# A gate pair with three Strassen units in place of four, one-piece splits of x1, a fourth raw weight tile

## Chip, cores and metric

One core of one Trainium2 chip. The metric is device time in microseconds (us), the median of several runs of the same program; the profile is of one further execution.

## The reference

One layer of a hybrid decoder block on 256 tokens of width 2048, all in float32:

```
h  = RMSNorm(x);  u = h @ w_in                     # 2048 x 12288, cut into c b xa za q f iv og ga gb
ya = b * conv3(c * xa) * silu(za)                  # 1024 wide
yb = RMSNorm_head(HGRN2(q, f, iv)) * silu(og)      # 1024 wide, 8 heads of 128
m  = sigmoid(ga) * (ya @ w_a) + sigmoid(gb) * (yb @ w_b)
x1 = x + m @ w_o                                   # 2048 x 2048
x2 = x1 + sigmoid(RMSNorm(x1) @ w_pg) * (p @ w_pp) # w_pg: 2048 x 2048
out = RMSNorm(x2)
```

The change acts on the last two products: the end of `m @ w_o`, and `x1 @ w_pg`.

## The kernel before, in words

Each product is cut into groups of 512 output columns. A group's contraction runs over chunks of 256 rows, each two tiles of 128 rows; the 256 tokens are two halves of 128. To keep float32 precision, every operand is split into a high part (rounded to the fp32r type) and a low part (the rest), and each product is made of three matmuls: high x high, high x low, low x high (`product`, L1147; inside a pair, `add`, L1169).

*Weights* come as a raw tile of two chunks (1 MB), loaded by SyncE's queue, SP (`load`, L103), with three raw tiles in rotation. `split` (L130) then makes, chunk by chunk, `whi` with one ScalarE copy (ACT, L151) and `wlo` with one VectorE subtraction (DVE, L152). Steps of the program are numbered; `ahead(pos)` says how many steps the splits run ahead of the matmuls, and `ask_ahead` asks for raw tiles. Four split buffers rotate; in the last stage, from the first step of `w_pg` on, six more in the pool `late`.

*Groups.* After the four groups of `w_o` (kind `O`) come those of `w_pg`: group 0 by itself (`PG` 0, eight steps), groups 1 and 2 as a pair (`GP`), and group 3 (`PG` 3) at the end, in which the first token half is done over all 512 columns, and the second half in two pieces of 256 columns. In a pair a chunk for both groups can be done as a *Strassen unit* ("S", chunk): seven block products where the plain way takes eight, from sums of weight blocks (`combine_weights`, L163 to L167, in place in the raw tile and in a half tile `t2`) and sums of blocks of x1 (`forms`). It takes four parts, one of them half a step wide. A plain unit (group, chunk) takes two chunks of one group, in two parts. The order is a list written out by hand, `LATE`.

*Epilogue of the pair.* `sums` (L765) waits until all products of a bank are made and adds the banks up (L761, L774); when gate 1, then gate 2 is whole, `gated` (L902) applies sigmoid (L908), the product with the kept projection `pw` (L911), the addition to the residual (L912) and the sum of squares (L913, L920). Of the PSUM banks with tag `g` there are four; the pair holds all four, so the last group's first bank is one that the additions have read.

*The O epilogue* (`ep_o`) adds the product to the residual, and turns x1 into feature-major layout (`turned`): four writes to DRAM (L294), one read back (L296), both from SP, then DVE's transpose (L300). For groups 0 and 1 of x1, four ACT scalings, one copy and one subtraction make the high and low parts, and `forms` the block sums. For groups 2 and 3 `put` does it in four scaled copies (L258) and four subtractions (L259).

*Tail.* `last_half` (L928 to L936) handles a piece of the last group, `sums_so_far` (L945 to L957) closes the sums of squares of the pieces before, `last_norm` (L966 to L985) scales and stores.

*What sets the order.* Each engine runs its instructions in one fixed order, which a scheduler lays down when the program is built, from the program's order, the pools' buffers and its own estimates. `advance` makes the epilogues' next steps after each step of matmuls, `issue_after` puts those behind the splits already issued.

Of the kernel before, what the change touches and what calls it, by code (L numbers as in the profile page):

```python
# [15 lines left out]
P = 128  # L16
# [25 lines left out]
GATES = ("S", 0), (0, 2), ("S", 1), (1, 2), ("S", 4), (0, 6), ("S", 5), (1, 6)  # L42
LATE = (0, 4), ("S", 0), (0, 6), ("S", 1), (1, 4), ("S", 2), ("S", 3), (1, 6)

# [7 lines left out]
def hybrid_kernel(ctx, tc, xT, x, pT, prm, gfin, masks, w_in, w_a, w_b, w_o, w_pg, w_pp, out):  # L52
# [44 lines left out]
    stream = []  # L97
    unit_of, part_of, joint = [], [], []
    loaded = {}
    parts = {}  # L100
    half = {}

    def load(pos):  # L103
        w, g, c = stream[pos]
        if unit_of[pos] not in loaded:
            raw = wp.tile([P, 2, 2 * CW], F32, tag="raw", bufs=3, name=nm("raw"))
            loaded[unit_of[pos]] = raw
            if joint[pos]:
                nc.sync.dma_start(out=raw[:, 0, :], in_=w[g, :, c, :])
                for i in range(2):  # L110
                    nc.sync.dma_start(
                        out=raw[:, 1, i * CW : (i + 1) * CW], in_=w[g + 1, :, c, (1 - i) * CW : (2 - i) * CW]
                    )
            elif FIRST <= pos < FIRST + 20:
                for i in range(2):
# [14 lines left out]
    def split(pos, c0=0, c1=2 * CW):  # L130
        part = part_of[pos]
        src = load(pos)[:, part % 2, :]
        if joint[pos]:

            src = load(pos)[:, part == 3, :]
            if part == 1:
                src, c1 = half[unit_of[pos]], CW

        pool, n = (pools["late"], 6) if (pos - state.get("late", len(steps))) % 10 < 6 and "late" in state else (wp, 4)
        if more(pos) and pos % (4 + MORE) < MORE:  # L140
            pool, n = pools[more(pos)], MORE
        if pos not in parts:
            parts[pos] = tuple(
                pool.tile([P, 2 * CW], F32R, tag=tag, bufs=n, name=nm(tag)) for tag in ("whi", "wlo")
            )
        hi, lo = parts[pos]
        s = slice(c0, c1)
        with ExitStack() as order:
            for i in state["before"].pop() if state.get("before") else ():
                order.enter_context(tc.issue_after(i))  # L150
            a = nc.scalar.activation(out=hi[:, s], in_=src[:, s], func=AF.Copy)  # L151
            v = nc.vector.tensor_tensor(  # L152
                out=lo[:, s], in0=src[:, s], in1=hi[:, s].bitcast(F32), op=ALU.subtract
            )
        state["splits"] = (a.ins, v.ins)
        if joint[pos] and part == 0:
            combine_weights(pos)
# [24 lines left out]
    active, done = [], 0  # L182
    def add_step(gi, c, w, g, k, part, s):
# [4 lines left out]
        joint.append(s)  # L188

    for gi, (kind, j, w, g, op, *program) in enumerate(groups):  # L190
# [4 lines left out]
        for n, (u, c) in enumerate(program[0]):  # L195
            for part in range(4 if u == "S" else 2):
                add_step(gi, (n, part), w, g if u == "S" else g + u, c if u == "S" else c + part, part, u == "S")

# [5 lines left out]
    gates, late = of_kind("GG"), of_kind("PG")[0]  # L204
    gates = range(gates[0] - 12, gates[-1] + 9)

# [77 lines left out]

    def turned(src, lag, dst=None):

# [8 lines left out]
        yield  # L295
        nc.sync.dma_start(out=src, in_=d.rearrange("p a x -> p (a x)"))  # L296
        for _ in range(lag):
# [424 lines left out]
    def forms(op, pool, tag, r, chunks):  # L722


        f = t4()
        a11, a12, a21, a22 = (r[:, :, k, t * P : (t + 1) * P] for t in range(2) for k in range(2))
        s1, s2, s3, s4 = (f[:, i * 2 * P : (i + 1) * 2 * P].rearrange("p (u t) -> p u t", u=2) for i in range(4))
        nc.vector.scalar_tensor_tensor(out=s1, in0=a21, scalar=-1.0, in1=a22, op0=ALU.mult, op1=ALU.subtract)
# [4 lines left out]
        yield  # L733
        hi, lo = (pool.tile([P, 1024], F32R, tag=tag + x, bufs=len(chunks) // 2, name=nm(tag + x)) for x in "hl")
        nc.scalar.activation(out=hi, in_=f, func=AF.Copy)
        nc.vector.tensor_tensor(out=lo, in0=f, in1=hi.bitcast(F32), op=ALU.subtract)
        for u in range(2):
            for i in range(4):
                s = slice((2 * i + u) * P, (2 * i + u + 1) * P)
                state["S", op, chunks[u], i] = hi[:, s], lo[:, s]  # L740
# [397 lines left out]
    def ahead(pos):  # L1138

        return LEAD + min(max(pos - late - 4, 0) // 3, 5) + MORE * (more(pos + LEAD) is not None and more(pos + LEAD + MORE) == more(pos + LEAD))  # L1140

# [54 lines left out]
    def products_of(program):  # L1196

        plain = [4 * sum(u == g for u, _ in program) for g in range(2)]
        joined = sum(u == "S" for u, _ in program)
# [204 lines left out]
```

## Time and profile before

| | |
|---|---|
| runs | 815.12 us median of 3 (814.78 to 815.52) |
| profiled execution | 814.94 us |
| its span, first to last instruction | 813.1 us |
| mean granted TensorE clock | 0.997 |
| TensorE (PE) busy | 802.5 us, 4196 matmuls |
| VectorE (DVE) busy | 629.6 us |
| ScalarE (ACT) busy | 465.2 us |
| GpSimd (POOL) busy | 91.1 us |
| DMA, mean over the span | 232 GB/s |

Places in the span: the `O` groups' matmuls end at 718.4 us, `PG` 0 runs from there to about 740, the pair to 781, the last group to 804.4. A row of an order of time has start, duration, engine, line, operation, tiles, and in brackets how long the engine had stood idle and what it waited for. A group row has, behind the first bar, busy time and the mean ns of one instruction, and behind the second the idle time before them. A window's row has, after its length, busy time and count of PE, PE's weight loads, DVE, ACT and POOL, then the clock, the DMA engines' share and GB/s.

### The profile page before, as it was taken

To read this page: it belongs to the slowest core of one execution; us is meant where nothing else is said; L and a number is where in the kernel's file an instruction comes from. 1 tells how busy PE (TensorE), PEld (TensorE's weight loads), DVE (VectorE), ACT (ScalarE), POOL (GpSimd) and SP (SyncE) were. 2 spreads that over 40 slices of the span, in tenths; PEclk is the share of its full clock that TensorE was granted. 3 is DMA by queue.
4 is the path that set the end of the run, shared out by engine and by line. 5 is a ranking of instruction groups with operands and counts; after the bars stand their busy time and mean duration, and the time that the engine had idled before them with its cause. 6 is when DMAs were issued, how large, how long until landed. Compare 5 with 4: busy or idle time off the path is not lost.

```text
span 813.1 us, 10989 instructions
## 1 busy us (share of the span) xinstructions
PE 802.5 (99%) x4196; PEld 666.9 (82%) x4196; DVE 629.6 (77%) x742; ACT 465.2 (57%) x609; POOL 91.1 (11%) x74
## 2 busy tenths in 40 slices
PE   9999999999999999999999999999999999999995
PEld 7888888888888888888888888888888888888875
DVE  5747697967766488967767998998997657779996
ACT  7667475555555465565664555564564456665653
POOL 1000045400000055200001000100100000001012
PEclk9999999999999999999999999999999999999998
DMA  9979656747767555647764774774766687887442
GB/s 337 366 281 338 226 172 206 228 172 237 258 233 256 186 183 202 213 156 264 269 238 148 224 272 144 248 257 157 259 236 230 213 300 257 283 315 252 165 181 105
DMA packets 46709, 188.33 MB, mean 232 GB/s; under 512 B 5312, under 2 KB 14784, under 8 KB 31552
## 3 DMA queue, kind: packets, MB, share of 16 engines
q1 hardware_dynamic: 46512, 187.36, 66.6%
q8 instruction: 33, 0.54, 0.3%
q10 hardware_dynamic: 144, 0.26, 0.1%
q14 instruction: 20, 0.16, 0.1%
HBM read 173.97 MB, written 13.63 MB: 231 GB/s over the span
## 4 chain that ended last, share of the span: by engine, by line
PE 90%; DVE 5%; DMA 1%; issue 1%; ACT 1%; POOL 0%; ACTq 0%; POOLq 0%; DVEq 0%
PE g L1147 73%; PE g L1169 11%; PE s L1169 4%; DVE wlo L152 2%; DMA raw<-in_w_pg 1%; PE s L1147 1%; PE s L450 1%; DVE t L911 1%; DVE raw L163 1%; DMA raw<-in_w_pp 0%; DVE xs L912 0%; ACT whi L151 0%; DVE t L929 0%; DVE t L761 0%; DVE t L166 0%
## 5 line engine op out<-in xcount | busy, mean ns | idle before, releaser
L152 DVE TENSOR_TENSOR wlo<-raw,whi 128x1024 fp32r<-128x1024 f32 (+1 forms) x311 | 385.1, 1254 | 154.3 <-ACT whi L151 153.0
L151 ACT ACTIVATE whi<-raw 128x1024 fp32r<-128x1024 f32 (+1 forms) x311 | 320.8, 1049 | 251.1 <-PE g L1147 195.6
L1147 PE MATMUL g<-whi,xh 128*128 128x512 f32 (+1 forms) x656 | 251.8, 385 | 0.6 <-DVE t L761 0.6
L1147 PE MATMUL g<-wlo,xh 128*128 128x512 f32 (+1 forms) x656 | 251.9, 384 | 0.0
L1147 PE MATMUL g<-whi,xl 128*128 128x512 f32 (+1 forms) x656 | 251.7, 384 | 0.0
L1147 PEld LDWEIGHTS g<-whi,xh 128*128 128x128 f32 x656 | 123.3, 188 | 25.2 <-DVE t L761 1.0
L1147 PEld LDWEIGHTS g<-whi,xl 128*128 128x128 f32 x656 | 123.3, 188 | 24.5
L1147 PEld LDWEIGHTS g<-wlo,xh 128*128 128x128 f32 x656 | 123.3, 188 | 24.2
L1169 PE MATMUL g<-wlo,xh 128*128 128x512 f32 x160 | 62.2, 389 | 0.0
L1169 PE MATMUL g<-whi,xl 128*128 128x512 f32 x160 | 62.2, 389 | 0.0
L1169 PE MATMUL g<-whi,xh 128*128 128x512 f32 x160 | 62.1, 389 | 0.0
L1147 PE MATMUL g<-whi,mh 128*128 128x512 f32 x128 | 49.8, 389 | 0.0
L1147 PE MATMUL g<-wlo,mh 128*128 128x512 f32 x128 | 49.8, 389 | 0.0
L1147 PE MATMUL g<-whi,ml 128*128 128x512 f32 x128 | 49.6, 389 | 0.0
L151 ACT ACTIVATE whi<-t 128x512 fp32r<-128x512 f32 x16 | 10.1, 630 | 53.7 <-DVE t L166 53.7
L1169 PEld LDWEIGHTS g<-whi,xh 128*128 128x128 f32 x160 | 30.0, 188 | 6.2
L1169 PEld LDWEIGHTS g<-wlo,xh 128*128 128x128 f32 x160 | 30.0, 188 | 6.2
L1169 PEld LDWEIGHTS g<-whi,xl 128*128 128x128 f32 x160 | 30.0, 188 | 6.2
L824 POOL TENSOR_TENSOR t<-ga,gb 128x512 f32<-128x512 f32 x6 | 10.6, 1780 | 193.0 <-issue 118.1
L1147 PE MATMUL g<-whi,yaTh 128*128 128x512 f32 (+1 forms) x74 | 28.0, 385 | 0.5 <-ACT whi L151 0.5
L1147 PEld LDWEIGHTS g<-whi,mh 128*128 128x128 f32 x128 | 24.0, 188 | 5.0
L1147 PEld LDWEIGHTS g<-wlo,mh 128*128 128x128 f32 x128 | 24.0, 188 | 5.0
(250 smaller groups left out, 931.4 us busy)
## 6 DMA issues: line engine op xcount, KB each, us to landing
raw<-in_w_in SPq DMA_DIRECT2D x73, 1024.0 KB, 4.9
raw<-in_w_in SPq DMA_DIRECT2D x34, 512.0 KB, 6.0
raw<-in_w_o SPq DMA_DIRECT2D x16, 1024.0 KB, 6.0
raw<-in_w_pg SPq DMA_DIRECT2D x12, 1024.0 KB, 6.1
turn<-t SPq DMA_DIRECT2D x72, 128.0 KB, 2.6
t<-turn SPq DMA_DIRECT2D x18, 512.0 KB, 5.1
raw<-in_w_a SPq DMA_DIRECT2D x8, 1024.0 KB, 5.3
raw<-in_w_b SPq DMA_DIRECT2D x8, 1024.0 KB, 5.4
```

The lines of the kernel that those rows point to most:

```text
L151: a = nc.scalar.activation(out=hi[:, s], in_=src[:, s], func=AF.Copy)
L152: v = nc.vector.tensor_tensor(out=lo[:, s], in0=src[:, s], in1=hi[:, s].bitcast(F32), op=ALU.subtract)
L163: nc.vector.tensor_tensor(out=b[:, 0:4:3, :], in0=b[:, 0:3:2, :], in1=b[:, 3:4, :].to_broadcast([P, 2, CW]), op=ALU.subtract)
L450: nc.tensor.matmul(heads(bk)[r, h, c if at is None else slice(at, at + 32)], key(h)[:, r], query(h)[:, c], start=True, stop=True, tile_pos ...
L824: (nc.vector if j == 3 else nc.gpsimd).tensor_tensor(out=spread(m, t), in0=blocks(ga[:, s]), in1=blocks(gb[:, s]), op=ALU.add)
L911: nc.vector.tensor_tensor(out=gt[:, s], in0=gt[:, s], in1=pw[:, s], op=ALU.mult)
L1147: nc.tensor.matmul(psum, a, b, start=first and n == 0, stop=last and n == 2)
L1169: nc.tensor.matmul(banks[name], x, y[:, s], start=k == total[name] and i == 0, stop=k == 1 and i == 2)
```

## The change

- In `LATE`, Strassen unit 3 goes. Its chunk is done plainly for both groups by a new kind of unit, (2, 3): part 0 is chunk 3 of group 1, part 1 is chunk 3 of group 2, loaded as two transfers of 512 KB (`across`). Plain unit (1, 4) moves behind the last Strassen unit.
- x1's splits are of one form for all four groups: four scalings, one copy, one subtraction. `forms` is made for the joined chunks alone, so for one chunk in place of two for x1's group 1.
- The read that brings x1 back from DRAM is issued by POOL in place of SP.
- A fourth raw tile (pool `tmp3`), used by every fourth unit from within the output projection on; `ask_ahead` asks one unit further there.
- From the eleventh step of the output projection on, a fifth split buffer in `tmp3` and one step more of lead. In the last stage four `late` buffers in place of six, with that fifth and the four others nine in rotation in place of ten; the lead grows by one every two steps from two steps before the stage in place of every three from four steps after it, to the same eight.

```diff
-LATE = (0, 4), ("S", 0), (0, 6), ("S", 1), (1, 4), ("S", 2), ("S", 3), (1, 6)
+LATE = (0, 4), ("S", 0), (0, 6), ("S", 1), (2, 3), ("S", 2), (1, 4), (1, 6)
...
     def load(pos):
-            raw = wp.tile([P, 2, 2 * CW], F32, tag="raw", bufs=3, name=nm("raw"))
+            pool, n = (pools["tmp3"], 1) if unit_of[pos] in fourth else (wp, 3)
+            raw = pool.tile([P, 2, 2 * CW], F32, tag="raw", bufs=n, name=nm("raw"))
...
+            elif across[pos]:
+                for i in range(2):
+                    nc.sync.dma_start(out=raw[:, i, :], in_=w[g + i, :, c, :])
...
-        pool, n = (pools["late"], 6) if (pos - state.get("late", len(steps))) % 10 < 6 and "late" in state else (wp, 4)
+        pool, n = (pools["late"], 4) if "late" in state and (pos - state["late"]) % 9 < 4 else (wp, 4)
+        if "late" in state and (pos - state["late"]) % 9 == 4 or pos in outs and pos % 5 == 4:
+            pool, n = pools["tmp3"], 1
...
-    gates = range(gates[0] - 12, gates[-1] + 9)
+    gates, outs = range(gates[0] - 12, gates[-1] + 9), range(of_kind("O")[0] + 10, late + LEAD + 1)
+    fourth.update(range(unit_of[outs[0]] // 4 * 4 + 7, unit_of[-1] + 1, 4))
...
-        nc.sync.dma_start(out=src, in_=d.rearrange("p a x -> p (a x)"))
+        (back or nc.sync).dma_start(out=src, in_=d.rearrange("p a x -> p (a x)"))
...
     def ep_o(j, psum):
-        turn = turned(x1, 2)
+        turn = turned(x1, 2, back=nc.gpsimd)
...
-        if j < 2:
-            for c in range(4):
-                h = x1[:, c * T : (c + 1) * T]
-                nc.scalar.activation(out=h, in_=h, func=AF.Identity, scale=gain(PRM_GPLE, j * 4 + c))
-            hi, lo = (x[:, j * 4 : j * 4 + 4, :].rearrange("p k t -> p (k t)") for x in state["x1T"])
-            nc.scalar.activation(out=hi, in_=x1, func=AF.Copy)
-            nc.vector.tensor_tensor(out=lo, in0=x1, in1=hi.bitcast(F32), op=ALU.subtract)
+        for c in range(4):
+            h = x1[:, c * T : (c + 1) * T]
+            nc.scalar.activation(out=h, in_=h, func=AF.Identity, scale=gain(PRM_GPLE, j * 4 + c))
+        hi, lo = (x[:, j * 4 : j * 4 + 4, :].rearrange("p k t -> p (k t)") for x in state["x1T"])
+        nc.scalar.activation(out=hi, in_=x1, func=AF.Copy)
+        nc.vector.tensor_tensor(out=lo, in0=x1, in1=hi.bitcast(F32), op=ALU.subtract)
+        joined = [c for u, c in LATE if u == "S" and c // 2 == j]
+        if joined:
             yield
-            r = x1.rearrange("p (u k t) -> p u k t", u=2, k=2)
-            yield from forms("x1T", pools["tmp3"], f"So{j}", r, (2 * j, 2 * j + 1))
-            return
-        for c in range(4):
-            put(state["x1T"], j * 4 + c, x1[:, c * T : (c + 1) * T], gain(PRM_GPLE, j * 4 + c))
+            r = x1.rearrange("p (u k t) -> p u k t", u=2, k=2)[:, : len(joined)]
+            yield from forms("x1T", pools["tmp3"], f"So{j}", r, joined)
...
     def ahead(pos):
-        return LEAD + min(max(pos - late - 4, 0) // 3, 5) + ...
+        return LEAD + (pos + LEAD in outs) + min(max(pos - late + 2, 0) // 2, 5 - (pos + LEAD in outs)) + ...
...
     def ask_ahead():
-            for u in range(unit_of[q], unit_of[q] + 2 + (part_of[q] > 0)):
+            for u in range(unit_of[q], unit_of[q] + 2 + (part_of[q] > 0) + (unit_of[q] - 1 > min(fourth))):
...
     def pair_products(at, program, opname):
+            q, k = (part, 2 * c) if u == 2 else (u, 2 * c + 2 * part)
             for i in range(2):
                 for t in range(NT):
-                    add((t, u), *tile_of(2 * c + 2 * part + i, t), (a, b)[i])
+                    add((t, q), *tile_of(k + i, t), (a, b)[i])
```

More of the change, by code (lines that the diff above doesn't have):

```diff
@@ L97, in hybrid_kernel @@
     stream = []
-    unit_of, part_of, joint = [], [], []
+    unit_of, part_of, joint, across = [], [], [], []
     loaded = {}
@@ L101, in hybrid_kernel @@
     half = {}
+    fourth = set()
     def load(pos):
@@ L182, in hybrid_kernel, with add_step @@
     active, done = [], 0
-    def add_step(gi, c, w, g, k, part, s):
+    def add_step(gi, c, w, g, k, part, s, a=False):
         stream.append((w, g, k))
@@ L188, in add_step @@
         joint.append(s)
+        across.append(a)
     for gi, (kind, j, w, g, op, *program) in enumerate(groups):
@@ L196, in hybrid_kernel @@
             for part in range(4 if u == "S" else 2):
-                add_step(gi, (n, part), w, g if u == "S" else g + u, c if u == "S" else c + part, part, u == "S")
+                if u == "S":
+                    add_step(gi, (n, part), w, g, c, part, True)
+                else:
+                    add_step(gi, (n, part), w, g + (part if u == 2 else u), c + part * (u < 2), part, False, u == 2)
     last_group = len(steps) - w_pg.shape[2]
@@ L283, in spread, with turned @@
         return ap.rearrange("p (b c t e) -> p t c b e", b=4, c=4, t=NT)[:, t]
-    def turned(src, lag, dst=None):
+    def turned(src, lag, dst=None, back=None):
         d = dram.tile([P, 4, T], F32, tag="turn", bufs=3, name=nm("turn"))
@@ L722, in forms @@
     def forms(op, pool, tag, r, chunks):
-        f = t4()
+        n = len(chunks)
+        f = t4()[:, : 4 * n * P]
         a11, a12, a21, a22 = (r[:, :, k, t * P : (t + 1) * P] for t in range(2) for k in range(2))
-        s1, s2, s3, s4 = (f[:, i * 2 * P : (i + 1) * 2 * P].rearrange("p (u t) -> p u t", u=2) for i in range(4))
+        s1, s2, s3, s4 = (f[:, i * n * P : (i + 1) * n * P].rearrange("p (u t) -> p u t", u=n) for i in range(4))
         nc.vector.scalar_tensor_tensor(out=s1, in0=a21, scalar=-1.0, in1=a22, op0=ALU.mult, op1=ALU.subtract)
@@ L733, in forms @@
         yield
-        hi, lo = (pool.tile([P, 1024], F32R, tag=tag + x, bufs=len(chunks) // 2, name=nm(tag + x)) for x in "hl")
+        hi, lo = (pool.tile([P, 4 * n * P], F32R, tag=tag + x, bufs=1, name=nm(tag + x)) for x in "hl")
         nc.scalar.activation(out=hi, in_=f, func=AF.Copy)
         nc.vector.tensor_tensor(out=lo, in0=f, in1=hi.bitcast(F32), op=ALU.subtract)
-        for u in range(2):
+        for u in range(n):
             for i in range(4):
-                s = slice((2 * i + u) * P, (2 * i + u + 1) * P)
+                s = slice((n * i + u) * P, (n * i + u + 1) * P)
                 state["S", op, chunks[u], i] = hi[:, s], lo[:, s]
@@ L1138, in ahead @@
     def ahead(pos):
-        return LEAD + min(max(pos - late - 4, 0) // 3, 5) + MORE * (more(pos + LEAD) is not None and more(pos + LEAD + MORE) == more(pos + LEAD))
+        return LEAD + (pos + LEAD in outs) + min(max(pos - late + 2, 0) // 2, 5 - (pos + LEAD in outs)) + MORE * (more(pos + LEAD) is not None and more(pos + LEAD + MORE) == more(pos + LEAD))
     def product(psum, op, k, t, hi, lo, first, last, which=(0, 1, 2)):
@@ L1196, in products_of @@
     def products_of(program):
-        plain = [4 * sum(u == g for u, _ in program) for g in range(2)]
+        plain = [sum(4 * (u == g) + 2 * (u == 2) for u, _ in program) for g in range(2)]
         joined = sum(u == "S" for u, _ in program)
```

## The prediction

> **What bounds the kernel now.** I read the page first, then the chain, then the order of time on TensorE (PE) from the last output projection to the end, and last what VectorE (DVE), ScalarE (ACT) and the queues did around the few places where PE was not fed.
>
> ```profile
> span 813.1 us, 10989 instructions
> PE 802.5 (99%) x4196; PEld 666.9 (82%) x4196; DVE 629.6 (77%) x742; ACT 465.2 (57%) x609; POOL 91.1 (11%) x74
> PE 90%; DVE 5%; DMA 1%; issue 1%; ACT 1%; POOL 0%; ACTq 0%; POOLq 0%; DVEq 0%
> ```
>
> PE is busy 99% of the span, and 90% of the chain is PE. The chain leaves PE near 740 us for DVE, which looks like a DVE-bound pair; whether PE really waited there is told only by its own order of time. First a row of the chain, 24 matmuls of a plain unit where nothing waits; then PE's rows at the end of the late pair, and the last matmul:
>
> ```profile
> 458.80 5.44 PE g L1169 x24
> ...
> 780.50 0.39 PE L1169 MATMUL g<-wlo,xh 128*128 128x512 f32 x1
> 780.73 0.39 PE L1169 MATMUL g<-whi,xl 128*128 128x512 f32 x1
> 781.69 0.50 PE L1147 MATMUL g<-whi,xh 128*128 128x512 f32 x1 [0.58 <-DVE t L761]
> 782.03 0.40 PE L1147 MATMUL g<-wlo,xh 128*128 128x512 f32 x1
> 782.27 0.40 PE L1147 MATMUL g<-whi,xl 128*128 128x512 f32 x1
> ...
> 804.14 0.28 PE L1147 MATMUL g<-whi,xl 128*128 128x256 f32 x1
> ```
>
> Two 512-column matmuls start 0.23 us apart (780.50 to 780.73; 5.44 us for 24 of them, 0.2267 each). Through the whole pair they keep that step, with one hole: 0.96 us from 780.73 to 781.69, so 0.74 lost, and 0.12 more in the slow step to 782.03 behind it. PE waits there for an addition of the pair's epilogue (L761), because the last group needs a bank that this addition reads. So DVE, the bound by the chain, costs PE only 0.86 us in the stage that the change rewrites. The other place is after the last matmul, which ends at 804.42, while the span ends at 813.1:
>
> ```profile
> 804.22 0.15 DVE L945 TENSOR_TENSOR ss<-ss 128x1 f32<-128x1 f32 x1
> ...
> 805.49 0.16 DVE L957 TENSOR_TENSOR xs<-tot,tot 128x1 f32<-128x1 f32 x1 [0.73 <-POOL tot L956]
> 805.56 0.42 DVE L929 TENSOR_TENSOR t<-t,pw 128x256 f32<-128x256 f32 x1
> 804.46 0.47 ACT L928 ACTIVATE t<-g,r2r 128x256 f32<-128x256 f32 x1
> 797.33 0.82 ACT L928 ACTIVATE t<-g,r2r 128x256 f32<-128x256 f32 x2
> ```
>
> ACT's last sigmoid is done at 804.93, but DVE takes it at 805.56: it still has the sums of earlier pieces to close, and these are late because the first token half's sigmoid ran at 797.33, though its products ended near 793 (48 matmuls of 0.2267 from 781.7 make 792.6). So 0.63 us is lost here to the same late epilogue.
>
> **The change, part by part.** The sum goes against the profiled execution: 814.94 us, of which 813.1 is the span and 1.8 lies around it; the runs' median, 815.12, is 0.18 above it. Most of the diff can gain nothing directly, since PE does not wait where it acts; it can only take away cover or add it.
>
> *One unit fewer.* A Strassen unit has 7 block products of three matmuls, 21; the same chunk done plainly for both columns groups has 24 (2 rows of 128 x 2 token halves x 2 groups x 3). Chunk 3 now takes 24: +3 x 0.2267 = **+0.68 us** on PE, on the path with certainty, since PE sets the pace there.
>
> *What DVE is relieved of.* Groups of the whole span (the mean of one instruction is the second number behind the bar), then three stretches:
>
> ```profile
> L152 DVE TENSOR_TENSOR wlo<-raw,whi 128x1024 fp32r<-128x1024 f32 (+1 forms) x311 | 385.1, 1254 | 154.3 <-ACT whi L151 153.0
> L151 ACT ACTIVATE whi<-raw 128x1024 fp32r<-128x1024 f32 (+1 forms) x311 | 320.8, 1049 | 251.1 <-PE g L1147 195.6
> ...
> L163 DVE TENSOR_TENSOR raw<-raw 128x1024 f32<-128x1024 f32 x16 | 20.5, 1284 | 0.4
> L167 DVE TENSOR_TENSOR raw<-raw,t 128x512 f32<-128x512 f32 x16 | 11.1, 692 | 0.5
> L166 DVE TENSOR_TENSOR t<-raw 128x512 f32<-128x512 f32 x16 | 11.1, 692 | 0.5
> L152 DVE TENSOR_TENSOR wlo<-t,whi 128x512 fp32r<-128x512 f32 x16 | 11.1, 691 | 0.7
> L151 ACT ACTIVATE whi<-t 128x512 fp32r<-128x512 f32 x16 | 10.1, 630 | 53.7 <-DVE t L166 53.7
> L911 DVE TENSOR_TENSOR t<-t,pw 128x512 f32<-128x512 f32 x6 | 4.9, 832 | 1.0 <-ACT t L908 1.0
> L912 DVE TENSOR_TENSOR xs<-xs,t 128x512 f32<-128x512 f32 x6 | 3.9, 682 | 0.0
> 718.00:740.00 22.00, 22.00 (x99) 18.22 (x98) 17.15 (x22) 14.08 (x21) 1.61 (x1) 1.00 0.90 316
> 740.00:760.00 20.00, 20.00 (x90) 16.57 (x89) 19.04 (x20) 11.02 (x16) 4.00 (x2) 1.00 0.52 174
> 760.00:780.00 20.00, 20.00 (x90) 16.57 (x89) 17.89 (x19) 12.33 (x14) 0.00 (x0) 1.00 0.63 234
> ```
>
> The unit's combination goes (1.28 + 0.69 + 0.69 = 2.67 us) and its splits shrink from three whole and a half (3 x 1.25 + 0.69 = 4.45) to two (2.51): 4.6 us less DVE work, out of 36.9 of 40 us busy from 740 to 780 (the third number of a window's row counts from PE, so DVE is 19.04 and 17.89). That turns a nearly full DVE into one with some 7 us to spare.
>
> *The order of the units.* Before, the last Strassen unit ends one plain unit (24 x 0.2267 = 5.44 us) ahead of the end of the pair; the first addition came only as that plain unit ended:
>
> ```profile
> 777.59 2.01 ACT L151 ACTIVATE whi<-raw 128x1024 fp32r<-128x1024 f32 x2 [2.72 <-DMA raw<-in_w_pg]
> 779.50 0.58 ACT L774 ACTIVATE t<-s 128x512 f32<-128x512 f32 x1
> 780.96 0.68 DVE L761 TENSOR_TENSOR t<-t,g 128x512 f32<-128x512 f32 x1
> ```
>
> The addition stands on DVE behind splits that stood behind a weight transfer, so it was some 5.5 us late (780.96 against 775.5, where unit S 3 ended: 780.95 less 5.44). In the new order two plain units of group 1 follow the last Strassen unit, 10.88 us; if the addition is as late again, it still comes 5.4 us before the last group asks for the bank. So the hole goes: **-0.74 - 0.12 = -0.86 us**. All of gate 1 and most of the additions move into these 10.88 us too; what is left after the pair is two additions and gate 2, about 4.4 us of DVE (2 x 0.68, 2 x 0.83 at L911, 2 x 0.68 at L912) beside the last group's first pass of 10.9 us. The first half's sigmoid then runs when its products end, the sums close early, and the last L929 starts when ACT is done: **-0.63 us**. If this cover is gone (DVE late again), both gains are gone, 1.49 us; that is a rival.
>
> *Fourth raw tile, fifth split buffer, more lead* (three steps ahead becomes four in the output projection, and the ramp to eight starts at the gate's first step; nine split buffers in rotation in place of ten). Cost: none on PE, where it did not wait before; what it moves is the transfers, which come earlier. The window from 718 to 740 has the DMA engines at 0.90 and 316 GB/s already, so it is there that an earlier 1 MB collides with something. I take nothing for it; the upper bound is in the rivals.
>
> *One-piece splits of x1 and the return read from POOL.* Four scaled copies with four subtractions per group become four scalings, one copy and one subtraction, for groups 2 and 3. Only group 3 is near the path: its last two chunks are what the first gate group (PG 0) waits for.
>
> ```profile
> 725.99 0.34 SPq L296 DMA_DIRECT2D t<-turn  x1
> 726.40 1.61 POOL L271 TENSOR_TENSOR r2r<-r2v,mhalf 128x2 f32<-128x2 f32 x1 [153.51 <-DVE r2v L267]
> 729.13 2.01 ACT L151 ACTIVATE whi<-raw 128x1024 fp32r<-128x1024 f32 x2 [3.63 <-DMA raw<-in_w_pg]
> 731.37 1.24 DVE L300 STREAM_TRANSPOSE t<-t 128x1024 f32<-128x1024 f32 x1
> 733.09 1.70 ACT L258 ACTIVATE xh<-t,prm_t 128x256 fp32r<-128x256 f32 x4
> 734.76 1.66 DVE L259 SCALAR_TENSOR_TENSOR xl<-t,prm_t,xh 128x256 fp32r<-128x256 f32 x4
> 736.53 0.39 PE L1147 MATMUL g<-whi,xh 128*128 128x512 f32 x1
> 737.89 0.62 PE L1147 MATMUL g<-whi,xl 128*128 128x512 f32 x2
> DMA to landing us min/median/max: 3.6/5.1/6.0
> SPq L296 <- DMA turn<-t: 10.5, 7, 2.2
> ```
>
> By the same start, the scalings end at 734.8, the copy (1.05, as a whole split's ACT half) at 735.8 and the subtraction (1.25) at 737.1. PE first used the high part at 736.53 and the low part at 737.89, with products of the pair's first unit put in front of them, so even the old order of PE has 0.7 us to spare. Against that stands the read that POOL now issues. No row of this trace has a transfer issued by POOL: from one side it is quicker than now, as SP's queue no longer holds it behind weight loads, by at most the 1.5 us between the median of 5.1 that such reads (L296) take to land and their least of 3.6; from the other it is slower by what POOL needs to start work, nearest row its 1.61 us power at 726.40. I take 0, with -1.5 and +1.6 us as ends; the 0.7 of slack and the pair's other products, of which more are split by then, should cover most of the latter. The 1.7 us of ACT that the dropped unit saves (3 x 1.05 + 0.63 less 2.1) pays for the two copies. SP gains the 10.5 us that its queue waits for writes from 600 on, with weight loads standing behind; as PE did not wait for weights, that is cover, not time.
>
> [...]
>
> [...]
>
> Sum: +0.68 - 0.86 - 0.63 = -0.81, so 814.94 becomes 814.1 in the profiled execution, **814.3 us** against the median.
>
> **The rivals.**
>
> *The epilogue is late all the same.* The scheduler may leave the additions behind the splits, with eight splits ahead of PE filling DVE's queue. Against it: 10.9 us of room and 4.6 us less work. For it: the old lateness came from a weight transfer, not from DVE's load alone. Then the stall and the tail stay and only the three matmuls count: 815.12 + 0.68 = 815.8 us.
>
> *PG 0 waits for x1 (the other side).* ACT takes group 3's scalings only behind the splits queued before them, and at 729.13 such a split had waited 3.63 us for its weights. With more lead, one more split may stand ahead of the scalings, and its weights compete with POOL's read at a DMA share of 0.90. If the scalings come a whole such wait later, x1 misses PE by 3.6 - 0.7 = 2.9 us: 814.3 + 2.9 = 817.2 us; with POOL's 1.6 on top 818.8. The point from which it counts as slower by over 0.2% (816.75) is 2.45 us of stall, thus 3.1 us of lateness. For it: the DMA rows above. Against it: the fourth raw tile lets those weights start earlier, and PE has two units' products to put in between, 5.44 and 4.76 us, if the program's fixed order on PE has them there.
>
> *The gain is more than counted.* Every other matmul stays, so the floor is the sum above less some of the 8.7 us after the last matmul. To be faster by over 0.2% (below 813.5) 0.8 us more would have to come out of that tail; nothing in the order above removes a step of it.
>
> **How the numbers follow.** 0.2% is 1.6 us, about what a measurement of this kernel can tell from no change. Forecast 0.51 (813.6 to 815.2), late epilogue 0.20 (815.3 to 816.5), x1 late 0.25 (mostly 816.8 to 818.8), more than counted 0.04. The first two are within 0.2%: 0.71. The range, 813.5 to 818.0 us, leaves out the last case and the worse half of the third, under 0.2 in all.
>
> **What would show it.** Right: 4199 matmuls; no hole over 0.3 us between the pair's last matmul (L1169) and the last group's first; the pair's first L761 some 5 us before the pair ends; the last L929 within 0.1 us of its sigmoid's end; DVE under 34 of the 40 us of the pair. Wrong: a gap on PE beside xh or xl of PG 0 with ACT or DMA as releaser (x1 late); L761 again as releaser of the last group (late epilogue); a gap in the output projection, which no step above allows.

## The result

| | before | after |
|---|---|---|
| median | 815.06 us (814.78 to 815.52, 6 runs) | 820.92 us (819.88 to 824.69, 6 runs) |
| profiled execution, its span | 814.94, 813.1 us | 824.69, 822.9 us |

The ratio is 1.0081, 95% interval 1.0058 to 1.0104: slower by 0.8%, 5.9 us by the medians, where 814.3 us was forecast. Lines after the change: splits L158 and L159, combination L170, L173, L174, x1's writes L306, read L308 and transpose L312, its scalings, copy and subtraction L870, L872, L873, POOL's root L283, the additions L774, gates L919 to L931, the last sigmoids L939 and L940, products L1158 (plain) and L1180 (pair).

The page of the kernel after, then all that PE waited for from 734 to 800 us (total, times, longest):

```profile
span 822.9 us, 11000 instructions
PE 808.4 (98%) x4199; PEld 670.2 (81%) x4199; DVE 621.6 (76%) x731; ACT 465.3 (57%) x609; POOL 94.0 (11%) x78
PE 87%; issue 4%; DMA 3%; ACT 3%; DVE 2%; SPq 0%; POOL 0%; POOLq 0%; ACTq 0%; DVEq 0%
...
PE g L1158 <- ACT xh L872: 3.7, 1, 3.7
PE s L1180 <- DVE wlo L159: 1.7, 2, 1.1
```

Two places, neither of which had a hole before: group PG 0 waits for x1's last part, and the pair's second Strassen unit waits for a split. The chain of waits has DMA at 3%, which had 1% before. PE in order of time at both places, and at the pair's end:

```profile
742.47 0.39 PE L1180 MATMUL g<-whi,xl 128*128 128x512 f32 x1
746.57 0.50 PE L1158 MATMUL g<-whi,xh 128*128 128x512 f32 x1 [3.72 <-ACT xh L872]
...
763.95 0.39 PE L1180 MATMUL s<-whi,So0h 128*128 128x512 f32 x1
765.39 0.50 PE L1180 MATMUL s<-wlo,So0h 128*128 128x512 f32 x1 [1.06 <-DVE wlo L159]
...
766.22 0.40 PE L1180 MATMUL g<-whi,xh 128*128 128x512 f32 x1
767.26 0.53 PE L1180 MATMUL s<-wlo,So0h 128*128 128x512 f32 x1 [0.64 <-DVE wlo L159]
...
792.11 0.39 PE L1180 MATMUL g<-whi,xl 128*128 128x512 f32 x1
792.34 0.39 PE L1158 MATMUL g<-whi,xh 128*128 128x512 f32 x1
```

Less the step of 0.23, the holes are 3.87, 1.21 and 0.81 us; the old hole in front of the last group is gone (792.11 to 792.34). Behind each place the windows show more; the first number is the length, then the busy times of PE, PEld, DVE, ACT and POOL, the granted clock, the DMA share and GB/s:

```profile
747.10:750.50 3.40, 3.40 (x9) 2.63 (x9) 3.40 (x4) 1.84 (x2) 0.00 (x0) 0.50 0.00 0
750.50:767.50 17.00, 15.30 (x66) 11.91 (x65) 14.74 (x16) 8.98 (x13) 4.28 (x2) 1.00 0.52 186
767.60:771.00 3.40, 3.40 (x9) 2.66 (x8) 3.40 (x4) 3.40 (x5) 0.00 (x0) 0.50 0.47 133
```

PE is busy in both stretches of 3.4 us, but at half the granted clock, so each costs 1.7 us. The profiled execution is 9.75 us longer than that of before: holes 5.89, half clock 3.4, the three matmuls 0.68, the old hole -0.86, the tail behind the last matmul -0.7 (8.0 us in place of 8.7), together 8.4. Another 1.0 lies in two small holes, ahead of 136 us and at 683.6, and 0.3 in the slow first step behind each of the three new holes (0.34 in place of 0.23 us). It is the longest of the six executions: those with a mean granted clock of 0.998 took 819.9 to 820.3 us, those at 0.993, like this one, 823.8 and 824.7. The first of these are what the forecast and the holes alone make, 814.3 + 5.89 = 820.2 us; so the loss that comes every time is the holes, and by their clocks the half clock comes on top in some executions.

Group 3 of x1 on its way, in order of time over all engines; the first row is from the kernel before:

```profile
721.11 2.15 SPq L294 DMA_DIRECT2D turn<-t  x4
...
725.54 1.78 SPq L306 DMA_DIRECT2D turn<-t  x4
...
732.40 1.62 POOL L283 TENSOR_TENSOR r2r<-r2v,mhalf 128x2 f32<-128x2 f32 x1 [21.24 <-DVE r2v L279]
733.99 0.57 POOL L308 DMA_DIRECT2D t<-turn  x1
741.64 1.25 DVE L312 STREAM_TRANSPOSE t<-t 128x1024 f32<-128x1024 f32 x1 [6.66 <-DMA t<-turn]
742.92 1.70 ACT L870 ACTIVATE t<-t,prm_t 128x256 f32<-128x256 f32 x4 [9.20 <-DVE t L312]
745.48 1.04 ACT L872 ACTIVATE xh<-t 128x1024 fp32r<-128x1024 f32 x1
```

The transpose comes 10.3 us later than before (741.64 against 731.37). From the first write to the read's issue 8.45 us pass, and POOL's queue has the root in front of the read; from the issue to the transpose 7.65, against 5.38 before. The rest, 4.4 us, is that the writes themselves come later (725.54, against 721.11 before). Groups 0 to 2 were read through POOL too, and in VectorE's (DVE's) order the additions for group 3 (L774, at 722.70) stand behind the late transpose of group 2 (at 719.29). All reads, by who issued them (times, KB, median us to landing):

```profile
t<-turn SPq DMA_DIRECT2D x14, 512.0 KB, 5.3
t<-turn POOLq DMA_DIRECT2D x4, 512.0 KB, 8.4
```

### The profile page after: what moved, and what is told of

Read it like the earlier page. It is cut to its first block, busy times and chain, and to the rows that moved or that the text cites. A ratio compares the mean times of both kernels' runs of the same rounds, so it can differ in the third digit from the quotient of the medians.

```text
span 822.9 us, 11000 instructions
## 1 busy us (share of the span) xinstructions
PE 808.4 (98%) x4199; PEld 670.2 (81%) x4199; DVE 621.6 (76%) x731; ACT 465.3 (57%) x609; POOL 94.0 (11%) x78
## 4 chain that ended last, share of the span: by engine, by line
PE 87%; issue 4%; DMA 3%; ACT 3%; DVE 2%; SPq 0%; POOL 0%; POOLq 0%; ACTq 0%; DVEq 0%
PE g L1158 66%; PE g L1180 13%; PE s L1180 5%; DMA t<-turn 3%; ACT whi L158 1%; PE s L1158 1%; PE s L462 1%; PE s L1036 1%; ACT t L870 0%; DMA turn<-t 0%; DVE wlo L159 0%; DVE t L312 0%; ACT xh L872 0%; ACT t L855 0%; DVE raw L170 0%
## 5 line engine op out<-in xcount | busy, mean ns | idle before, releaser
L159 DVE TENSOR_TENSOR wlo<-raw,whi 128x1024 fp32r<-128x1024 f32 (+1 forms) x310 | 383.6, 1255 | 142.1 <-ACT whi L158 140.8
L158 ACT ACTIVATE whi<-raw 128x1024 fp32r<-128x1024 f32 (+1 forms) x310 | 319.5, 1049 | 233.3 <-PE g L1158 189.9
L1158 PE MATMUL g<-whi,xh 128*128 128x512 f32 (+1 forms) x656 | 252.4, 386 | 3.7 <-ACT xh L872 3.7
L1158 PE MATMUL g<-wlo,xh 128*128 128x512 f32 (+1 forms) x656 | 252.4, 385 | 0.0
L1158 PE MATMUL g<-whi,xl 128*128 128x512 f32 (+1 forms) x656 | 252.3, 385 | 0.0
L1158 PEld LDWEIGHTS g<-whi,xh 128*128 128x128 f32 x656 | 123.5, 188 | 28.7 <-ACT xh L872 4.1
L1158 PEld LDWEIGHTS g<-whi,xl 128*128 128x128 f32 x656 | 123.7, 189 | 24.8
L1158 PEld LDWEIGHTS g<-wlo,xh 128*128 128x128 f32 x656 | 123.6, 188 | 24.0
L1180 PE MATMUL g<-wlo,xh 128*128 128x512 f32 x166 | 64.8, 390 | 0.0
L1180 PE MATMUL g<-whi,xl 128*128 128x512 f32 x166 | 64.8, 390 | 0.0
L1180 PE MATMUL g<-whi,xh 128*128 128x512 f32 x166 | 64.6, 389 | 0.0
L1158 PE MATMUL g<-wlo,mh 128*128 128x512 f32 x128 | 49.9, 390 | 0.3 <-DVE wlo L159 0.3
L1158 PE MATMUL g<-whi,mh 128*128 128x512 f32 x128 | 49.8, 389 | 0.0
L1158 PE MATMUL g<-whi,ml 128*128 128x512 f32 x128 | 49.6, 389 | 0.0
L158 ACT ACTIVATE whi<-t 128x512 fp32r<-128x512 f32 x15 | 9.5, 632 | 54.0 <-DVE t L173 54.0
L1180 PEld LDWEIGHTS g<-whi,xl 128*128 128x128 f32 x166 | 31.3, 189 | 6.5
L1180 PEld LDWEIGHTS g<-wlo,xh 128*128 128x128 f32 x166 | 31.3, 189 | 6.5
L1180 PEld LDWEIGHTS g<-whi,xh 128*128 128x128 f32 x166 | 31.2, 188 | 6.5
L312 DVE STREAM_TRANSPOSE t<-t 128x1024 f32<-128x1024 f32 x16 | 19.8, 1240 | 21.0 <-DMA t<-turn 21.0
L1158 PEld LDWEIGHTS g<-wlo,mh 128*128 128x128 f32 x128 | 24.0, 188 | 5.7 <-DVE wlo L159 0.7
L1158 PE MATMUL g<-whi,yaTh 128*128 128x512 f32 (+1 forms) x74 | 28.3, 389 | 0.0
```

The source lines that it names most:

```text
L159: v = nc.vector.tensor_tensor(out=lo[:, s], in0=src[:, s], in1=hi[:, s].bitcast(F32), op=ALU.subtract)
L312: nc.vector.transpose(out=dst.rearrange("p (k a e) -> p a k e", a=4, e=32), in_=src.rearrange("p (a k e) -> p a k e", a=4, e=32))
L1158: nc.tensor.matmul(psum, a, b, start=first and n == 0, stop=last and n == 2)
L1180: nc.tensor.matmul(banks[name], x, y[:, s], start=k == total[name] and i == 0, stop=k == 1 and i == 2)
```

## Experiments

Diffs are from the kernel after unless another is named. "SP's read" is x1's return read from SP as in the kernel before.

**Which part of the change costs what**

*SP's read in the kernel after.*

```
-        turn = turned(x1, 2, back=nc.gpsimd)
+        turn = turned(x1, 2)
```

> The change whole, but x1's read back from DRAM issued by SP again. Theory 1 (the read's way: POOL computes the root first, and with SP's queue free the weight loads take the DMA engines from it): the hole of 4.1 us on PE in front of x1's last chunks goes or stays under 0.5 us, no matmuls at half pace after it, and the time is what the sum said, 814 to 815 us. Theory 2 (the deeper prefetch itself, four raw tiles and the earlier lead, delays x1 through ACT and the DMA engines): a hole of 3 us or more stays, 818 us or more.

Measured: 816.81 us (9 runs), ratio 1.0025 [1.0015, 1.0034]. PE's waits from 734 to 800, x1's read and transpose, and then the chain:

```profile
PE s L1180 <- DVE wlo L159: 1.7, 2, 0.9
...
725.45 0.33 SPq L308 DMA_DIRECT2D t<-turn  x1
731.06 1.24 DVE L312 STREAM_TRANSPOSE t<-t 128x1024 f32<-128x1024 f32 x1
...
735.20 5.44 PE g L1180 x24
...
742.00 4.77 PE g L1158 x21
```

The wait for xh is gone, and 4.1 us of the 5.9 with it; x1's last writes start at 721.02 again, so the 4.4 us of late writes came with the reads from POOL. Against this kernel, the writes of the four groups start 1.0, 7.6, 5.7 and 4.5 us later in the kernel after. The two holes of the Strassen unit stay, so the time lies between what the two theories expected. The chain's rows, read again below, show the pair's matmuls from 735.20 to 742.00 in front of PG 0's last ones: 6.8 us, 30 of them.

*The kernel before, with the read from POOL alone* (`turned(x1, 2, back=nc.gpsimd)`).

> The kernel before with one part of the change alone: x1's read issued by POOL. Theory 1: x1's last chunks come 4 us or more later, PE waits 3 us or more in front of them and runs at half pace after it: 818 to 822 us. Theory 2: the read itself is harmless, 814.3 to 815.8 us.

Measured: 824.13 us (4 runs), 1.0112 [1.0096, 1.0129]. PE at PG 0 waits again, here for the high part (L258 there):

```profile
743.08 0.80 PE L1147 MATMUL g<-whi,xh 128*128 128x512 f32 x1 [4.63 <-ACT xh L258]
```

By the medians this one argument costs the old kernel 9.0 us, more than the whole change; but the two intervals just overlap, and all four executions had a granted clock of 0.992 to 0.995, so part of it may be half clock.

*The kernel after with the old buffers and lead, the read from POOL kept* (three raw tiles, ten split buffers, three steps of lead and the old ramp).

> The change with the old buffers and lead: three raw tiles, four split buffers and six late ones, the old ramp; x1's read still from POOL. Theory 1: still slow, 818 to 822 us, as the root still stands before the read. Theory 2: the hole goes, 814 to 815.5 us.

Measured: 824.95 us (820.37 to 826.34, 4 runs), 1.011 [1.008, 1.014]; PE waits 5.6 us for xh in its profile. So the deeper prefetch isn't what makes x1 late. Whether it softens the wait (5.6 us without it, 3.72 with it, one profile each) the times don't show: their intervals overlap.

*The same with SP's read: of the change only the three units, their order and the one-piece splits are left.*

> Of the change only the unit order with three Strassen units and the one-piece splits: x1's read from SP, old buffers, old lead. In the run with the read from SP two holes of 1.0 us each were left in the second Strassen unit, where DVE's order puts a combination of the third unit between those of the second. Theory B (the fourth raw tile lets that third unit's work in so early): with three raw tiles no hole, and the sum of the prediction comes true: 814.0 to 814.7 us, the last L929 within 0.1 us of its sigmoid. Theory A (POOL's multiplication slows DVE there): the holes stay, 815.5 to 817 us.

Measured: 814.53 us (11 runs), 0.9991 [0.9983, 1.0]. No wait of PE from 734 to 800. PE at the pair's end, the pair's first addition, and the last sigmoid with the product behind it:

```profile
775.51 0.68 DVE L771 TENSOR_TENSOR t<-t,g 128x512 f32<-128x512 f32 x1
781.75 0.39 PE L1177 MATMUL g<-whi,xl 128*128 128x512 f32 x1
781.98 0.39 PE L1155 MATMUL g<-whi,xh 128*128 128x512 f32 x1
804.57 0.47 ACT L936 ACTIVATE t<-g,r2r 128x256 f32<-128x256 f32 x1 [3.86 <-PE g L1155]
805.07 0.42 DVE L937 TENSOR_TENSOR t<-t,pw 128x256 f32<-128x256 f32 x1 [1.51 <-ACT t L936]
```

The addition comes 6.5 us ahead of the last group, the hole is gone, and DVE takes the last sigmoid when it ends. That fits the forecast's sum: -0.72 us against the runs of before beside it (815.25), -0.81 forecast, with an interval that just reaches no change.

**Why POOL's read is late**

*POOL's read put in front of the root.*

```
-        (back or nc.sync).dma_start(out=src, in_=...)
+        state["read"] = (back or nc.sync).dma_start(out=src, in_=...).ins
...
-            state["rstd2"] = rsqrt_of(tot, NT, D, "r2")
+            with tc.issue_after(state["read"]):
+                state["rstd2"] = rsqrt_of(tot, NT, D, "r2")
```

> The change whole, with one edit: POOL issues the last x1 read before it computes the root r2r, not after. Theory 1: the read is issued near 730 in place of 734.0, about 4 us earlier; it still shares the DMA engines with the weights (7 to 9 us to land), so the hole shrinks from 3.9 us lost to under 1 us: 815 to 817.5 us. If the root's place is no part of it: as the change, 820 to 824 us.

Measured: 817.76 us (6 runs), 1.0029 [1.0016, 1.0041].

```profile
723.40 1.78 SPq L306 DMA_DIRECT2D turn<-t  x4
728.55 0.53 POOL L308 DMA_DIRECT2D t<-turn  x1 [19.17 <-ACT whi L158]
737.03 1.25 DVE L312 STREAM_TRANSPOSE t<-t 128x1024 f32<-128x1024 f32 x1 [3.13 <-DMA t<-turn]
...
728.00:737.00 9.00, 9.00 (x42) 7.44 (x41) 4.53 (x6) 2.41 (x3) 2.15 (x2) 1.00 1.01 380
```

The read is issued 5.15 us behind the first write, much as before (4.88), so the root was 3.3 of the 3.6 us. It still takes 8.5 us to the transpose, in a window whose DMA share is 1.01. Of the wait for xh 0.3 us is left in the profile; the time lies just above the range expected. The writes start at 723.40, 2.3 us late in place of 4.4: the root's place made part of that lateness too, and the runs don't show by which way.

*The same, and SP held by a small read of the turned tile until its writes have landed.*

> The change with POOL's read ahead of the root, and SP's queue held as before: behind x1's writes SP issues a read of 32 numbers per partition of them, so its weight loads wait for the writes again. If the read is slow to land (7 us and more) because SP's weight loads run free: it lands in 5 to 6 us, and x1's transpose comes at 734 or before, with no hole in front of x1's last chunks: 816 to 817.5 us. If a read issued by POOL is slow by itself: 7 us or more, and 817 to 819 us.

Measured: 817.17 us (10 runs), 1.003 [1.0019, 1.0041]. The read is issued at 728.64 and the transpose starts at 736.62, 8.0 us; SP's loads start again at 726.66 and run beside it. Holding SP for the writes doesn't help. That was the outcome expected if a read from POOL is slow by itself, but the loads still ran beside it; the next run takes them away.

*The read in front of the root, and SP's weight loads held until each such read has landed* (SP copies 32 columns of the tile that was read to memory, and the loads stand behind that copy).

> The change with POOL's read ahead of the root, and SP held until each of x1's reads has landed (SP copies 32 numbers per partition of the tile away, and its weight loads stand behind that). A look at the read's landing alone, not at the time. If it took 8 us because SP's loads share the DMA engines with it: it lands in 4 to 5.5 us now. If a read issued by POOL is slow by itself: 7 us or more. The time should be worse than the kernel before, as weights come late.

Measured: 821.91 us, one run. The loads come late now, and PE waits for weights' splits, so its time says nothing of the read; the read does:

```profile
734.12 0.53 POOL L312 DMA_DIRECT2D t<-turn  x1 [19.99 <-DMA turn<-t]
737.72 1.25 DVE L319 STREAM_TRANSPOSE t<-t 128x1024 f32<-128x1024 f32 x1 [2.00 <-DMA t<-turn]
...
734.00:738.00 4.00, 4.00 (x19) 3.34 (x18) 2.00 (x3) 0.27 (x1) 2.15 (x2) 1.00 0.36 131
```

With nothing else in flight (131 GB/s for 4 us are the read's own 512 KB; share 0.36) it takes 3.6 us. The three earlier groups' reads in this run, with more still in flight, took 7.7, 7.7 and 5.2 us at shares of 0.77, 0.69 and 0.57. So POOL's issue isn't slow; the time went with what else was in flight. In the kernel before, SP's read took 5.38 us at a share of 0.98, where POOL's took 7.65 at 1.02. The two together say that the read is slow because, outside SP's queue, it no longer stands in front of SP's loads but shares the DMA engines with them. In the kernel before SP issued its next loads from 726.43 on, behind the read at 725.99; in the kernel after from 727.42 on, ahead of POOL's read at 733.99. The times fit, 3.6 us alone against 7.65 to 8.5 beside loads; how the DMA engines divide their time between two queues no run shows.

**Why the Strassen unit waits**

With SP's read the two holes stay. DVE and POOL before them, in that kernel:

```profile
747.57 1.32 DVE L922 TENSOR_TENSOR t<-t,pw 128x512 f32<-128x512 f32 x2 [0.49 <-ACT t L919]
750.38 4.24 POOL L931 TENSOR_TENSOR xs<-xs,gfin_t 128x512 f32<-128x512 f32 x2 [20.95 <-ACT t L924]
751.26 2.21 DVE L170 TENSOR_TENSOR raw<-raw 128x1024 f32<-128x1024 f32 x1
753.39 2.31 DVE L159 TENSOR_TENSOR wlo<-raw,whi 128x1024 fp32r<-128x1024 f32 x1
```

The unit's combination and a split take 2.2 and 2.3 us where such an instruction takes 1.2, while POOL multiplies group 0 by its gain. POOL's two instructions end at 752.39 and 754.62, DVE's two at 753.47 and 755.70, each 1.08 us behind one of POOL's. One theory (A) is that POOL's multiplication slows DVE there; others are that a fourth raw tile (B), nine split buffers instead of ten (B') or the earlier ramp of the lead (C) set DVE's order so.

*SP's read, and the old ramp* (`min(max(pos - late - 4, 0) // 3, ...)`).

> The change with the read from SP and the old ramp of the lead (the fourth raw tile and nine split buffers kept). Theory C (the early ramp fills all nine buffers, DVE then stands idle for 5.6 us and has the second Strassen unit's work late): the holes go, 814.2 to 815 us. Theories A and B: as with the read from SP alone, 816 to 817 us, since DVE's order around the second unit is the same.

Measured: 816.71 us (12 runs), 1.0019 [1.001, 1.0027], holes as before: not C alone.

*SP's read, and three raw tiles* (L106's `fourth` left out).

> The change with the read from SP and three raw tiles as before (nine split buffers and the early ramp kept). Theory B (the fourth raw tile lets the third unit's work in early): no hole, 814 to 815 us. Theory B' (it is the nine split buffers in place of ten that make the scheduler put the third unit's combination inside the second's; DVE's order still has it so here): the holes stay, 816 to 817 us.

Measured: 816.81 us (10 runs), 1.002 [1.0011, 1.003], holes as before: not B alone.

*Three raw tiles and ten split buffers* (from the last one).

> As the run with three raw tiles, but with ten split buffers in rotation (five late ones), the early ramp kept; in DVE's order the third unit's combination stands behind the second's parts. Theory B': no hole in the second unit, 814 to 815 us. If the ramp or the unit order itself is to blame: 816 us or more.

Measured: 816.69 us (10 runs), 1.0017 [1.0008, 1.0026]. DVE's queue no longer mixes the next unit's combination into this one's, and two holes are still there, 0.9 us each (the first now ends with ACT's `whi`, the second with DVE's `wlo`): not B' either.

*SP's read, and group 0's multiplication meant to come ten steps later* (eleven yields in front of it).

> The change with the read from SP, and POOL's multiplication of gate group 0 (L931) put off by ten steps, out of the second Strassen unit's combination. DVE's order is the same as without. Theory A: DVE's L170 there takes 1.2 us in place of 2.2 and the split behind it 1.2 in place of 2.3, the two holes (2.3 us) go: 814.2 to 815 us. Theory B: about 1 us of hole stays: 815.5 to 816.5 us.

Measured: 816.6 us (11 runs), 1.002 [1.0012, 1.0029]. The edit didn't do what it says: the multiplication still starts at 749.93, where its inputs are ready. It tells nothing.

*SP's read, and group 0's multiplication by the gain left out.*

```
-            nc.gpsimd.tensor_tensor(out=d, in0=d, in1=state["gfin"][:, ...], op=ALU.mult)
+            if j:
+                nc.gpsimd.tensor_tensor(out=d, in0=d, in1=state["gfin"][:, ...], op=ALU.mult)
```

> The change with the read from SP, and POOL's multiplication by the last norm's gain left out for columns 0 to 511 (two instructions of L931; the output lacks that factor there). DVE's order stays. Theory A (POOL beside DVE): L170 takes 1.2 us in place of 2.2 and the split behind it 1.2 in place of 2.3, so the second Strassen unit's parts are some 2 us earlier and the two holes (2.3 us lost) go or keep under 0.4 us: 814.3 to 815 us. Theory B' (DVE's order, in which the third unit's combination is put inside the second's): about 1 us of hole stays, 815.3 to 816.3 us.

The output lacks that factor in columns 0 to 511. Measured: 814.74 us (10 runs), 0.999 [0.998, 1.0]; DVE has the same order, and PE waits for nothing there:

```profile
750.94 1.22 DVE L170 TENSOR_TENSOR raw<-raw 128x1024 f32<-128x1024 f32 x1
752.08 1.22 DVE L159 TENSOR_TENSOR wlo<-raw,whi 128x1024 fp32r<-128x1024 f32 x1
```

That is A: 1.22 us each in place of 2.21 and 2.31, 2 us of DVE, 2.1 us of time. By what way POOL's instruction slows DVE's the runs don't show. But the kernel before has the same multiplication beside DVE, and no hole:

```profile
742.71 1.33 DVE L911 TENSOR_TENSOR t<-t,pw 128x512 f32<-128x512 f32 x2 [0.82 <-ACT t L908]
746.89 4.00 POOL L920 TENSOR_TENSOR xs<-xs,gfin_t 128x512 f32<-128x512 f32 x2 [18.88 <-ACT t L913]
749.77 2.19 DVE L163 TENSOR_TENSOR raw<-raw 128x1024 f32<-128x1024 f32 x1
```

With SP's read it comes 3.5 us later, because gate 0 starts at 747.57 and not at 742.71. That fits TensorE's order: 30 matmuls of the pair in front of PG 0's last 24, where the kernel before has 10 in front of or among them and the one with the order alone 19; 20 x 0.2267 = 4.5 of the 4.9 us. The same order holds up DVE in a second way: before 745.85 it stands idle for 5.58 us, as ACT's next copy waits 6.38 us for PG 0's products.

*SP's read, with the pair's matmuls behind its first 12 held back until PG 0's last.*

```
+            with ExitStack() as behind:
+                if kind == "GP" and c >= (0, 1):
+                    behind.enter_context(tc.issue_after(state["pg"]))
+                pair_products(c, program, opname)
```

> The kernel after with x1's read from SP, and with all of the pair's matmuls behind its first 12 held back on TensorE until the first gate group's last one, so that 12 of them and not 30 stand in front of that group's last 24. If TensorE's order is what makes gate 0 late, its first addition to pw comes 18 x 0.2267 = 4.1 us earlier than 747.57, near 743.5, POOL's multiplication starts near 746.3 and ends near 750.6, before the second Strassen unit's combination on VectorE; that and the split behind it take 1.2 us each again, no hole is left and the time is 814.4 to 814.9 us. If the holes have another cause (weights, buffers, VectorE's own order), they stay, 1.7 us, and the time is 816.5 to 817. A third way: group 0 now asks for x1 18 matmuls earlier, and a hole of up to 2 us comes at its xh or xl.

Measured: 814.45 us (11 runs), 0.9988 [0.998, 0.9997]. Its chain, and DVE and POOL:

```profile
735.18 2.72 PE g L1180 x12
737.90 5.44 PE g L1158 x24
...
743.47 1.33 DVE L922 TENSOR_TENSOR t<-t,pw 128x512 f32<-128x512 f32 x2 [0.49 <-ACT t L919]
746.29 4.23 POOL L931 TENSOR_TENSOR xs<-xs,gfin_t 128x512 f32<-128x512 f32 x2 [16.87 <-ACT t L924]
747.17 2.19 DVE L170 TENSOR_TENSOR raw<-raw 128x1024 f32<-128x1024 f32 x1
749.40 1.66 DVE L173 TENSOR_TENSOR t<-raw 128x512 f32<-128x512 f32 x1
```

Gate and multiplication come when the expectation has them (743.5, 746.3) and no hole is left. One detail was wrong: the combination moved along and still lies beside POOL (2.19 and 1.66 us). It is early enough now to bear that. DVE's idle time ahead of gate 0 shrank as well, to 1.51 us, so the run doesn't separate the two ways in which TensorE's order holds DVE up.

*The same with 24 in front* (`c >= (1, 0)`).

> The same with 24 of the pair's matmuls in front of the first gate group's last 24 (the pair's whole first unit). By TensorE's order, POOL's multiplication starts 6 x 0.2267 = 1.4 us earlier than 750.38, near 749.0, and ends near 753.2: the Strassen unit's combination still takes 2.2 us, but the split behind it 1.2, so half of the loss goes: holes of 0.6 us or less and 815.0 to 815.9 us. If TensorE's order is not the cause, holes of 1.7 us and 816.5 to 817.

Measured: 814.33 us (11 runs), 0.9989 [0.998, 0.9998]: all of the loss went, not half. In its trace gate 0 comes 1.1 us earlier than with 30 (746.51), and DVE's queue has no combination of the next unit between this one's. So lateness adds up from TensorE's order, DVE's order and POOL: 2 us less from POOL is enough, and so is 1.1 us less from TensorE with DVE's queue unmixed. This kernel and the one with 12 in front are faster than the kernel before by 0.1%, with intervals that just leave out no change.

## Why the prediction was wrong

Two losses stand between 814.3 and 820.9 us, and one of them was a rival: 814.3 + 4.1 (x1) + 2.3 (Strassen unit; 816.81 with it, 814.53 without) = 820.7.

- **The failed step is "I take 0"** for the read that POOL issues, with ends of -1.5 and +1.6 us and 0.7 us of slack. Group 3's transpose came 10.3 us later. The upper end priced POOL's start as a thing beside the read, but the 1.61 us root stood in the prediction's own rows, 0.4 us behind the old read; with the read on POOL the two share a queue, and the read was issued 3.6 us later behind its writes, 3.3 of them for the root in front. The second link was read with the wrong sign: SP's loads standing behind the read were its protection. Its lower end, the read quicker off SP's queue, never came; 5.4 became 7.65 us. The third I didn't ask for at all: groups 0 to 2 go the same way, and late transposes make the next group's write late, 4.4 us.
- **The rival "PG 0 waits for x1"** had the place, the releaser and the price (2.9 to 4.5 us of stall; the hole is 3.87, the loss by medians 4.1). Its mechanism was another: ACT's scalings start 1.3 us behind the transpose; the read was late, not ACT's queue. Its chance, 0.25, was too low for a price whose nearest rows said nothing of a second queue at a DMA share of 0.90.
- **The second loss was not foreseen.** "It can only take away cover or add it" was said of buffers and lead, and only DMA was priced. The cover that went was time: TensorE's order pushed gate 0, and the splits that wait for PG 0's products, back by 20 matmuls. That POOL's multiplication slows DVE was to be seen in the trace before (2.19 us at L163 beside it, 1.23 at 759.74 without); that the order would change was not.
- **Right:** 4199 matmuls, no hole in front of the last group, the tail. With both losses out, the sum measured -0.72 us for -0.81. The last rows of the tail in the kernel after itself:

```profile
814.93 0.47 ACT L939 ACTIVATE t<-g,r2r 128x256 f32<-128x256 f32 x1 [5.22 <-PE g L1158]
815.43 0.42 DVE L940 TENSOR_TENSOR t<-t,pw 128x256 f32<-128x256 f32 x1 [2.87 <-ACT t L939]
```

- **Wrong, without effect:** DVE under 34 of 40 us. With the order alone it is 35.9 from 740 to 780 (18.11 and 17.82 in the windows): three of the pair's additions have moved into that stretch (2.1 us), and 20 whole splits start in it where there were 21 before. Its busy time over the whole span did fall, by 8.0 us (629.6 to 621.6).
- **What stays open:** why the program's ordering puts 30 matmuls in front. The kernels with SP's read that kept some of the added lead or buffers, and whose order was not set by an edit, have 30; all of these keep the fifth split buffer and the extra step of lead from the output projection on, which no run took out alone. The kernel with none of them has 19 with SP's read, but 30 with POOL's, so the added prefetch isn't the only thing that does it.

## What to carry to other kernels

A transfer that the next product waits for did best here in the queue that also carries the bulk loads, ahead of them (5.38 us to the transpose): moved to an idle engine's queue it shared the DMA engines with those loads (7.65 us; 3.6 in the run that held them back), and it waited in order for what that engine computes (the root of 1.62 us, which put off its issue by 3.3). When a change moves transfers or buffers, look not only for transfers that collide but for what the fed engine will now do earlier, and whose work that pushes back. And price an edit on a helper by all its calls in the chain: one group's delay can start the next group late.

## What the hardware showed unexpectedly

- After a hole of 3.87 us TensorE ran 3.4 us at a granted clock of 0.50, and again after holes of 1.21 and 0.81 us within 3.3 us. The second pair is 2.02 us together, about half of the first hole, and got a stretch of the same length, in this execution. With SP's read two holes of 1.0 and 1.06 us, 1.9 us apart, got none in the profiled execution. What starts such a stretch, and what sets its length, these traces don't show. Such a stretch costs 1.7 us; executions at a granted clock of 0.995 with SP's read took 818.8 and 818.9 us, the others (0.996 to 0.998) 816.4 to 816.9.
- The same 512 KB read from POOL took 3.6 us alone and 7.65 to 8.5 beside weight loads; from SP, ahead of the loads, 5.38.
- A DVE instruction of 1024 elements with two SBUF inputs took 1.22 us, and 2.2 to 2.3 in the places above, beside POOL's multiplication of group 0; two of them cost 2.1 us of DVE and, by the medians, 2.1 us of the kernel. POOL's multiplication, 1.30 us with DVE idle (at 798.65 in the kernel after), took 2.0 to 2.3 there. With SP's read, DVE's split before the pair ends at 751.23; then POOL, DVE, POOL, DVE end at 752.39, 753.47, 754.62 and 755.70, steps of 1.08 to 1.16. So the two took turns there, and next to nothing of them overlapped. In the traces of before, of after, of SP's read, of the order alone and of 12 and 24 matmuls in front, such a DVE instruction ended 1.07 to 1.09 us behind POOL's. Elsewhere it was POOL that took longer: in the kernel after its two multiplications from 791.63 on took 4.43 us, beside DVE's two splits from 791.28 on in 2.36; with SP's loads held until the read had landed, those of group 0 took 8.86 us from 753.72 on, beside three splits in 3.49. What decides which of them waits, these traces don't show.
